# Macaron block in fp32: roots of two norms placed sooner, squares from feature tiles, 24 triples ahead of the pairs, output projection by four blocks, compression jobs spread

## The chip, the cores and the metric

One core of a Trainium2 chip. Its engines run side by side and wait for each other by semaphores: TensorE (PE) does matmuls, its weight loads are listed apart (PEld); VectorE (DVE) and ScalarE (ACT) do elementwise work, ScalarE also activations; GpSimd (POOL) helps with elementwise work; SyncE (SP) issues the DMAs. The metric is the device time of one execution, in microseconds (us).

## The reference

Batch 1, S = 512 tokens, D = 1024 features, all in fp32. One block: half of a SwiGLU FFN, a mixer, half of a second FFN, a final norm.

```
x = x + 0.5 * swiglu(rmsnorm(x, norm_ffn1), gate, up, down)          # D_FF = 2816
x = x + hybrid_mixer(rmsnorm(x, norm_mix), ...)
x = x + 0.5 * swiglu(rmsnorm(x, norm_ffn2), gate, up, down)
out = rmsnorm(x, norm_final)

rmsnorm(x, g) = x * rsqrt(mean(x*x) + eps) * g
swiglu(h) = (silu(h @ w_gate) * (h @ w_up)) @ w_down
```

The mixer projects h by `w_in` into queries, keys and values of 16 heads of 64. Heads 0 to 7 attend in blocks of 256 (MoBA). Heads 8 to 15 (NSA) sum three attentions with gates: over keys and values compressed by a small MLP (31 positions; the code calls its parts k/v `proj`, `hid`, `sec`), over selected blocks, and over a window. The 16 outputs are concatenated and multiplied by `w_out` (1024 x 1024).

## The kernel before

**Layout.** x lies in eight feature tiles `x0` to `x7` (128 features x 512 tokens). fp32 products are made of three matmuls of a rounded type (`mm3`, L86 to L88): high by high, high by low, low by high part. Every operand is split for it: ACT makes the high part (L80 for weights, L196 for other data), DVE the low part (L81, L197); in the mixer POOL takes L81 of small weights. For the norms, x times the gain is split into `xo` (`gained`, L122 on ACT and L123 on DVE), and the root R of a token is multiplied in later. Squares of x are summed over the feature tiles into `acc` (L134, L137 on ACT, the add L138), `sums_of_squares` adds over the partitions by matmuls with ones (`pr`, L144), `roots` gives 1/rms, and `rows_of_roots` spreads it over a 128x512 tile R (`pR`, L155, copied by ACT at L157).

**FFN.** D_FF is 22 columns f of 128. The first four f are `plain`: 16 steps of 12 matmuls (2.72 us of PE by the code's own table), eight with feature tiles 0 to 3 and eight with 4 to 7. Then `finish` makes h from the two banks: two products with R (L260), Silu, a product (L262), and `kept` splits h into high part (L224) and low part (L225). The other 18 f are taken two at a time by `pair`, seven products of sums of blocks in the manner of Strassen and Winograd (14 steps of 1.36 us). They need sums of x's blocks, which DVE makes out of x, the gain and R: `sums_of_x` (L186 to L190) and `blocks_of_x`, entered by `x_sums` at numbered plain steps. The weights' sums (`aw`, L288) and splits (L196, L197) are DVE and ACT work too. `down` multiplies four h by `w_down` in triples of matmuls (0.68 us): for a pair of output tiles d first k = 0, 1, 2 of both, then k = 3 of both; the bank is added to x at L464. There are 32 triples for the four plain h. `LEAD` of them come right behind the plain steps; the rest is mixed into the first pairs. So the steps are: plain, LEAD triples, then pairs mixed with triples.

**What sets the order.** Inside an FFN, PE's order is the list of steps (`go`), which also calls each step's loads, sums and splits 26, 12.8 and 8.6 us of PE ahead; the other engines' order, and all engines' in the mixer, comes from the Tile scheduler, from simulated times. A function attached to a step (`post`) is placed behind it: roots, rows of roots, sums of x, and in FFN1 `put_rows` and copies of bias tables.

**FFN1's roots** come from four tiles of x by tokens (`in_x`, 512 KB each), squared by ACT with a running sum (L510).

**Mixer.** A list of jobs (`pre`, `fill`, `last`) is run by `stream`, which loads the weights of a job two jobs ahead into three buffers and splits them before use. `pre` holds the first projections and the compression (`kproj`, `khid`, `ksec`, `vproj`, `vhid`, `vsec`) and values by tokens (`vn`, `vm`). Then come the heads, 8 to 15, then 0 to 7: each in chunks, of which scores (`ps_s`, L874, L875; bias and maximum L880; exponential L882; reciprocal L884; scaling by POOL L889), transposes (`ps_t`, L898; split L901, L902) and values (`po`, L92, L93; halves L829 to L833) lag by 0, 4 and 7 chunks. Between these, `run` takes pieces of the `fill` jobs to keep PE busy. The last fills are MoBA's queries and keys (`pp`; t L590, L592; aq L599; ak L606 and a DMA that shifts it across partitions), two projections for two heads. The output projection `w_out(d, k0, k1)` multiplies blocks k0 to k1 (two heads each) for tile d and adds the bank to x (L784); a job of it may start only when its heads are done. In the order of before there are 32 such jobs of two blocks: (4,6) and (6,8) are NSA's, (0,2) is MoBA's heads 0 to 3, and (2,4), heads 4 to 7, are the `last`, eight jobs of six matmuls. Behind the last job for d comes its `gained` and `squares` for FFN2.

## Time and profile before

| | us |
|---|---|
| median of 3 runs | 1030.15 (1029.23 to 1030.98) |
| the profiled execution's own time | 1029.65 |
| its span, first to last instruction | 1027.9 |
| PE busy | 983.8 (96%) |
| DVE, ACT, POOL busy | 769.0, 528.6, 140.0 |
| mean granted clock of PE | 0.986 |

How its lines are read: a timeline row has the start, the time, the engine, the line of the code, the operation, output <- input by the program's names, the shape, and in brackets how long the engine was idle just before it and what ended that. A row of groups has the count behind x, then busy us, mean ns of one, and idle us. A row by windows has, for PE, PEld, DVE, ACT and POOL, busy us and instructions, then PE's granted clock (1.00 is full), the DMA's share and GB/s.

### The profile page before, as it was taken

The numbers are of one execution on the slowest core, as the hardware profiler recorded it, in microseconds if no ns is written. First come the engines' busy times: TensorE is split into PE (matmuls) and PEld (weight loads), VectorE is DVE, ScalarE is ACT, GpSimd is POOL, SyncE is SP. The second block draws the span as 40 slices with busy tenths as digits, with TensorE's granted clock in tenths as the row PEclk, the third lists the DMA queues.
The fourth block names the chain that finished last, engine by engine and source line by source line (L and its number), as shares of the span: only waits on it lengthen the run. The fifth ranks groups of instructions, "written<-read, shape, count | busy, mean of one in ns | idle before, by whom it ended". The sixth has DMA issues, their size and how long they took to land.

```text
span 1027.9 us, 15964 instructions
## 1 busy us (share of the span) xinstructions
PE 983.8 (96%) x6088; PEld 866.3 (84%) x6088; DVE 769.0 (75%) x1242; ACT 528.6 (51%) x913; POOL 140.0 (14%) x184
## 2 busy tenths in 40 slices
PE   9969999999999998999999999896999999999996
PEld 7848999999999897787877787685899999999985
DVE  4995776777766586688698989969677777677745
ACT  7733444444444255467577876646344444444336
POOL 0000000000000040046443645600000000000002
PEclk9989999999999999999999999998999999999999
DMA  9527433233321126531011322552333333342202
GB/s 325 204 71 225 129 123 101 90 110 94 100 82 41 45 75 184 179 105 52 16 42 26 99 57 79 154 197 89 103 101 104 95 95 101 124 123 62 62 1 82
DMA packets 43569, 106.55 MB, mean 104 GB/s; under 512 B 9410, under 2 KB 18323, under 8 KB 43493
## 3 DMA queue, kind: packets, MB, share of 16 engines
q1 hardware_dynamic: 43204, 105.39, 32.4%
q8 instruction: 48, 0.79, 0.3%
q14 instruction: 29, 0.23, 0.1%
q10 hardware_dynamic: 288, 0.14, 0.1%
HBM read 100.08 MB, written 5.30 MB: 103 GB/s over the span
## 4 chain that ended last, share of the span: by engine, by line
PE 51%; DVE 7%; issue 2%; ACT 2%; DMA 2%; POOL 0%; ACTq 0%; DVEq 0%; POOLq 0%; SPq 0%
PE pd L87 4%; PE pd L88 4%; PE pd L86 4%; PE pu L86 3%; PE pu L87 3%; PE pu L88 3%; PE pp L86 3%; PE pp L87 3%; PE pp L88 3%; PE pw L86 3%; PE pw L88 2%; PE pw L87 2%; PE ps_t L898 2%; PE pgu L88 1%; PE pgu L86 1%
## 5 line engine op out<-in xcount | busy, mean ns | idle before, releaser
L196 ACT ACTIVATE sph<-aw 128x1024 fp32r<-128x1024 f32 x126 | 133.7, 1061 | 263.3 <-PE pu L87 117.4
L197 DVE TENSOR_TENSOR spl<-aw,sph 128x1024 fp32r<-128x1024 f32 x126 | 153.6, 1220 | 35.8 <-ACT sph L196 35.8
L87 PE MATMUL pd<-h,whi 128*128 128x512 f32 x336 | 135.5, 403 | 16.1 <-DVE h L225 16.1
L80 ACT ACTIVATE whi<-raw 128x1024 fp32r<-128x1024 f32 (+3 forms) x125 | 108.7, 872 | 71.5 <-PE pd L87 24.9
L86 PE MATMUL pd<-h,whi 128*128 128x512 f32 x336 | 134.5, 400 | 1.1 <-DVE x L464 0.7
L88 PE MATMUL pd<-h,wlo 128*128 128x512 f32 x336 | 133.2, 396 | 0.0
L86 PE MATMUL pu<-th,sph 128*128 128x256 f32 x432 | 120.5, 279 | 0.5
L88 PE MATMUL pu<-th,spl 128*128 128x256 f32 x432 | 120.1, 278 | 0.0
L87 PE MATMUL pu<-tl,sph 128*128 128x256 f32 x432 | 120.0, 278 | 0.0
L81 DVE TENSOR_TENSOR wlo<-raw,whi 128x1024 fp32r<-128x1024 f32 (+3 forms) x84 | 102.2, 1219 | 23.6 <-ACT whi L80 19.7
L288 DVE TENSOR_TENSOR aw<-aw 128x1024 f32<-128x1024 f32 x72 | 87.7, 1219 | 24.2 <-DMA aw<-in_wgu 24.1
L464 DVE SCALAR_TENSOR_TENSOR x<-pd,x 128x512 f32<-128x512 f32 x88 | 60.2, 687 | 50.8 <-PE pd L88 50.7
L86 PEld LDWEIGHTS pu<-th,sph 128*128 128x128 f32 x432 | 81.1, 188 | 6.8 <-ACT wc L304 2.3
L87 PEld LDWEIGHTS pu<-tl,sph 128*128 128x128 f32 x432 | 81.6, 189 | 4.3
L87 PEld LDWEIGHTS pd<-h,whi 128*128 128x128 f32 x336 | 64.4, 192 | 23.4 <-DVE h L225 18.6
L88 PEld LDWEIGHTS pu<-th,spl 128*128 128x128 f32 x432 | 81.1, 188 | 0.0
L88 PE MATMUL pw<-xo,spl 128*128 128x256 f32 x288 | 79.8, 277 | 0.0
L86 PE MATMUL pw<-xo,sph 128*128 128x256 f32 x288 | 79.8, 277 | 0.0
L87 PE MATMUL pw<-xo,sph 128*128 128x256 f32 x288 | 79.8, 277 | 0.0
L88 PEld LDWEIGHTS pd<-h,wlo 128*128 128x128 f32 x336 | 64.4, 192 | 14.2
L86 PEld LDWEIGHTS pd<-h,whi 128*128 128x128 f32 x336 | 64.1, 191 | 7.6 <-ACT h L224 1.1
L81 POOL TENSOR_TENSOR wlo<-raw,whi 128x256 fp32r<-128x256 f32 (+1 forms) x41 | 47.6, 1163 | 69.6 <-ACT whi L80 68.7
(252 smaller groups left out, 2462.4 us busy)
## 6 DMA issues: line engine op xcount, KB each, us to landing
aw<-in_wgu SPq DMA_DIRECT2D x72, 512.0 KB, 3.7
raw<-in_wd1a SPq DMA_DIRECT2D x20, 512.0 KB, 4.1
raw<-in_wd2a SPq DMA_DIRECT2D x20, 512.0 KB, 3.7
raw<-in_w_a SPq DMA_DIRECT2D x16, 512.0 KB, 3.6
raw<-in_wgu SPq DMA_DIRECT2D x15, 512.0 KB, 6.6
raw<-in_w SPq DMA_DIRECT2D x8, 512.0 KB, 3.9
raw<-in_w_o SPq DMA_DIRECT2D x32, 128.0 KB, 2.1
scr_t<-scr_r SPq DMA_DIRECT2D x8, 384.0 KB, 6.1
```

The lines of the kernel that those rows point to most:

```text
L80: nc.scalar.activation(hi[:, s], src[:, s], AF.Copy)
L81: (nc.gpsimd if side[0] else nc.vector).tensor_tensor(lo[:, s], src[:, s], f32(hi[:, s]), ALU.subtract)
L86: nc.tensor.matmul(p, w[0], v[0], start=first, stop=False, skip_group_check=again)
L87: nc.tensor.matmul(p, w[0], v[1], start=False, stop=False, skip_group_check=again)
L88: nc.tensor.matmul(p, w[1], v[0], start=False, stop=last, skip_group_check=again)
L196: nc.scalar.activation(hi, v, AF.Copy)
L197: nc.vector.tensor_tensor(lo, v, f32(hi), ALU.subtract)
L288: nc.vector.tensor_tensor(to, x, y, op)
L464: nc.vector.scalar_tensor_tensor(xs[d], p, 0.5, xs[d], ALU.mult, ALU.add)
L898: nc.tensor.transpose(p[:, wide:wide + 128], lps[qi][:, j * 128:(j + 1) * 128], ident)
```

## The change

1. `LEAD` is 24 for 8, in both FFNs.
2. FFN1's sums of squares are made from the feature tiles: `squares` for each of the eight (ACT, and the seven adds on DVE), then `pr`. The four token tiles, their loads and the input `x` go. `pr` is placed behind plain step 3, R's rows (`pR`) behind step 4 (before: 5), the sums of x from step 5 on (before: 6).
3. FFN2: `pr` behind step 2 (before 3), `pR` behind 3 (before 5), the sums of x from step 4 (before 6).
4. `put_rows` goes from the end of the lead triples to the 19th pair step, the bias copies from pair steps 4 + 5i to 26 + 3i.
5. The compression's hidden jobs are spread among other jobs of `pre`, their bank has another tag, `vsec` is last.
6. The output projection has 16 jobs of four blocks: (4,8) for each d, in the fill at i = 2, and (0,4) for each d as the `last`. There is one add into x per job, and one split of 128x512 weights in place of two of 128x256.

```diff
-LEAD = 8
+LEAD = 24
-    def x_sums(ffn):
-        return [(at, lambda k=k, part=part: part(k)) for k, ats in enumerate(((6, 6), (8, 8), (10, 10), (13, 15)))
+    def x_sums(ffn, first):
+        return [(at, lambda k=k, part=part: part(k))
+                for k, ats in enumerate(((first, first), (first + 1, 8), (first + 3, 10), (first + 5, 15)))
                 for at, part in zip(ats, (ffn.sums_of_x, ffn.blocks_of_x))]
...
-        tokens = [ffn.raw().rearrange("p a b c -> p (a b c)") for _ in range(NT)]
-        for i in range(NT):
-            nc.sync.dma_start(tokens[i], A["x"][i * 128:(i + 1) * 128])
...
-        def squares_of_tokens():
-            for i in range(NT):
-                nc.scalar.activation(tokens[i], tokens[i], AF.Square, accum_out=ss[:, 0, i:i + 1])
-            roots(0, ss[:, 0])
+        def squares_of_x():
+            for k in range(NK):
+                squares(tmp, k, "tmp", 3, nc.vector)
...
         steps = ffn.plain(range(FP), [
-            (1, squares_of_tokens), (5, lambda: rows_of_roots(0, "mm")), (8, make_rows),
-            *x_sums(ffn)])
+            (0, squares_of_x), (3, lambda: roots(0, sums_of_squares("mm"))), (4, lambda: rows_of_roots(0, "mm")),
+            (8, make_rows), *x_sums(ffn, 5)])
         fills = ffn.down(A["wd1a"][0], range(FP), half_added, "mm", 2)
         steps += fills[:LEAD]
-        steps[-1].post.append(put_rows)
...
+        pairs[18].post.append(put_rows)
         for i in range(8):
-            pairs[4 + 5 * i].post.append(lambda i=i: copied_bias(i))
+            pairs[26 + 3 * i].post.append(lambda i=i: copied_bias(i))
...
-                        p.append(pt("mm", "pc"))
+                        p.append(pt("t", "pc"))
...
-                if k1 == 4:
+                if k0 == 0:
                     got["x", d] = gained(d, 2)
...
-        pre = [kproj, *vn, proj(10, nsa_k("ks")), *khid[:2], vm[0], *khid[2:], vproj, vm[1], ksec, vm[2],
-               *vhid, vsec, vm[3], proj(12, nsa_q(0))]
+        pre = [kproj, *vn, khid[0], proj(10, nsa_k("ks")), khid[1], vm[0], khid[2], vproj, khid[3], vm[1], ksec,
+               vhid[0], vm[2], vhid[1], vhid[2], vm[3], vhid[3], proj(12, nsa_q(0)), vsec]
...
             if i == 2:
-                fill += [w_out(d, 4, 6) for d in range(NK)]
-        fill += [w_out(d, k, k + 2) for k in (6, 0) for d in range(NK)]
-        last = [w_out(d, 2, 4) for d in range(NK)]
+                fill += [w_out(d, 4, 8) for d in range(NK)]
+        last = [w_out(d, 0, 4) for d in range(NK)]
...
         steps = ffn.plain(range(FP), [
-            (3, lambda: roots(2, sums_of_squares("mm"))), (5, lambda: rows_of_roots(2, "mm")), *x_sums(ffn)])
+            (2, lambda: roots(2, sums_of_squares("mm"))), (3, lambda: rows_of_roots(2, "mm")), *x_sums(ffn, 4)])
```

How it moves instructions is seen at three places. In the order's rows names carry the tile's number; the changed kernel's lines stand a few lower (L784 is L781 there, L874 L871, L898 L895, L902 L899).

DVE in FFN1, before, up to the low part of the last of the four plain h (`h_575` and `h_617` are h2 and h3; the rows of h0 and h1 stand 15 and 10 rows ahead of `h_575`):

```order
L260 TENSOR_TENSOR t_611<-pgu_329,R_100 128x512
L260 TENSOR_TENSOR t_611<-pgu_370,R_100 128x512
L288 TENSOR_TENSOR aw_423<-aw_425,aw_423 128x1024
L189 SCALAR_TENSOR_TENSOR xb_546<-xb_546 128x256
L197 TENSOR_TENSOR tl3_130<-xa_545,th3_129 128x256
L225 TENSOR_TENSOR h_575<-t_569,h_574 128x512
L262 TENSOR_TENSOR t_611<-t_611 128x512
L288 TENSOR_TENSOR aw_443<-aw_423,aw_443 128x1024
L197 TENSOR_TENSOR tl3_130<-xb_546,th3_129 128x512
L225 TENSOR_TENSOR h_617<-t_611,h_616 128x512
```

The same place now (`h_547`, `h_592` and `h_629` are h1, h2 and h3):

```order
L262 TENSOR_TENSOR t_586<-t_586 128x512
L81 TENSOR_TENSOR wlo_647<-raw_511,whi_646 128x1024
L225 TENSOR_TENSOR h_547<-t_541,h_546 128x512
L189 SCALAR_TENSOR_TENSOR xb_491<-xb_491 128x256
L197 TENSOR_TENSOR tl3_130<-xa_490,th3_129 128x256
L288 TENSOR_TENSOR aw_570<-aw_550,aw_570 128x1024
L262 TENSOR_TENSOR t_623<-t_623 128x512
L225 TENSOR_TENSOR h_592<-t_586,h_591 128x512
L197 TENSOR_TENSOR tl3_130<-xb_491,th3_129 128x512
L225 TENSOR_TENSOR h_629<-t_623,h_628 128x512
```

The low parts of h1, h2 and h3 now stand close together; h1's has the sums and splits of x's blocks ahead of it that stood behind it before.

PE in the mixer, before, at the last head's transposes (`ps_t`) and values (`po`); `pw` is the output projection, and `o60` to `o71` are outputs of heads finished long before:

```order
L898 MATMUL ps_t_6667<-ident_84,lpn_6535 128x128
L898 MATMUL ps_t_6667<-ident_84,lp_6556 128x128 x2
L93 MATMUL po_6705<-tl_6626,vm_4222 128x512
L92 MATMUL po_6705<-th_6645,vm_4223 128x384
L93 MATMUL po_6705<-tl_6646,vm_4223 128x384
L86 MATMUL pw_6882<-o60_5562,whi_6850 128x512
L87 MATMUL pw_6882<-o61_5563,whi_6850 128x512
L88 MATMUL pw_6882<-o60_5562,wlo_6851 128x512
L86 MATMUL pw_6882<-o70_5968,whi_6850 128x512
L87 MATMUL pw_6882<-o71_5969,whi_6850 128x512
L88 MATMUL pw_6882<-o70_5968,wlo_6851 128x512
L898 MATMUL ps_t_6696<-ident_84,lpn_6575 128x128
```

Now, at the last head's scores and transposes (`kvn_6738` and `kvn_6739` are the output of heads 4 and 5, halves of one block):

```order
L871 MATMUL ps_s_6746<-ak_6576,aq_6590 128x384
L872 MATMUL ps_s_6746<-ak_6578,aq_6590 128x384
L895 MATMUL ps_t_6755<-ident_84,lpn_6634 128x128
L895 MATMUL ps_t_6776<-ident_84,lpn_6634 128x128
L871 MATMUL ps_s_6767<-ak_6576,aq_6590 128x512
L872 MATMUL ps_s_6767<-ak_6578,aq_6590 128x512
L895 MATMUL ps_t_6755<-ident_84,lpn_6671 128x128
L895 MATMUL ps_t_6776<-ident_84,lpn_6671 128x128
L87 MATMUL pw_6861<-kvn_6739,whi_6505 128x512
L88 MATMUL pw_6861<-kvn_6738,wlo_6506 128x512
L87 MATMUL pw_6886<-kvn_6739,whi_6538 128x512
L88 MATMUL pw_6886<-kvn_6738,wlo_6539 128x512
```

The jobs (0,2) and (6,8) that stood between are gone from there; what is left is the beginning of the last jobs, up to the block whose heads are done.

DVE at the end of the mixer, before: the add of the last blocks into x (L784), and the low part of x times the gain (L123):

```order
L784 TENSOR_TENSOR x0_70<-pw_7022,x0_70 128x512
L784 TENSOR_TENSOR x1_71<-pw_7041,x1_71 128x512
L123 SCALAR_TENSOR_TENSOR xo_7031<-x0_70,gcol_69,xo_7030 128x512
L784 TENSOR_TENSOR x2_72<-pw_7062,x2_72 128x512
L123 SCALAR_TENSOR_TENSOR xo_7050<-x1_71,gcol_69,xo_7049 128x512
L784 TENSOR_TENSOR x3_73<-pw_7083,x3_73 128x512
L123 SCALAR_TENSOR_TENSOR xo_7071<-x2_72,gcol_69,xo_7070 128x512
L784 TENSOR_TENSOR x4_74<-pw_7104,x4_74 128x512
```

Now:

```order
L781 TENSOR_TENSOR x0_70<-pw_6861,x0_70 128x512
L781 TENSOR_TENSOR x1_71<-pw_6886,x1_71 128x512
L123 SCALAR_TENSOR_TENSOR xo_6876<-x0_70,gcol_69,xo_6875 128x512
L123 SCALAR_TENSOR_TENSOR xo_6901<-x1_71,gcol_69,xo_6900 128x512
L781 TENSOR_TENSOR x2_72<-pw_6913,x2_72 128x512
L123 SCALAR_TENSOR_TENSOR xo_6928<-x2_72,gcol_69,xo_6927 128x512
L781 TENSOR_TENSOR x3_73<-pw_6940,x3_73 128x512
L123 SCALAR_TENSOR_TENSOR xo_6955<-x3_73,gcol_69,xo_6954 128x512
```

Engine and rows are of one kind as before; what has changed is that each add stands for a bank of 12 matmuls in place of six, and that a first add of the same tile, for the blocks (0,2), no longer comes ahead.

More of the change, by code (lines that the diff above doesn't have):

```diff
@@ L1173, in _laid_out @@
         "gcol": c(np.stack([g[0].reshape(NK, 128).T for g in (norm_ffn1, norm_mix, norm_ffn2)], axis=1)),
-        "x": c(x[0]), "wgu1": _gate_up(w_ffn1_gate[0], w_ffn1_up[0]),
+        "wgu1": _gate_up(w_ffn1_gate[0], w_ffn1_up[0]),
         **dict(zip(("wd1a", "wd1b"), _down(w_ffn1_down[0]))),
```

## The prediction

> **What bounds the kernel now.** I read the page's head first, then busy time in stretches of 25 us, then TensorE's timeline for its gaps, then what the other engines do inside those gaps.
>
> ```profile
> span 1027.9 us, 15964 instructions
> PE 983.8 (96%) x6088; PEld 866.3 (84%) x6088; DVE 769.0 (75%) x1242; ACT 528.6 (51%) x913; POOL 140.0 (14%) x184
> ```
>
> TensorE (PE) is busy for 983.8 of 1027.9 us: the bound is its work plus 44.1 us of gaps. The change takes no matmul of weight away, so it can only win gaps, open new ones, or change the clock in them. Where they are:
>
> ```profile
> 0.00:25.00 25.00, 22.79 (x88) 17.82 (x89) 11.99 (x22) 18.49 (x30) 0.81 (x8) 1.00 0.92 324
> 50.00:75.00 25.00, 16.40 (x72) 11.50 (x70) 24.36 (x36) 8.62 (x14) 0.00 (x0) 0.80 0.20 65
> 400.00:425.00 25.00, 21.90 (x111) 17.64 (x110) 16.38 (x25) 12.11 (x18) 0.00 (x0) 1.00 0.50 156
> 552.00:668.00 116.00, 109.23 (x577) 89.71 (x576) 105.02 (x242) 84.31 (x198) 64.60 (x87) 1.00 0.31 89
> 648.00:668.00 20.00, 15.94 (x66) 11.61 (x65) 18.75 (x19) 14.45 (x24) 14.86 (x13) 1.00 0.58 177
> 700.00:725.00 25.00, 17.12 (x62) 13.11 (x62) 24.64 (x36) 10.95 (x18) 0.00 (x0) 0.80 0.22 73
> 750.00:775.00 25.00, 24.86 (x181) 22.95 (x180) 17.66 (x20) 10.92 (x15) 0.00 (x0) 1.00 0.37 116
> ```
>
> Columns: window and its length, then busy us of PE, weight loads, DVE, ACT and POOL, PE's granted clock, DMA share and GB/s. In the body of an FFN PE has no gap worth naming (750:775). One hole stands in each FFN where the plain part ends (8.6 and 7.9 us, the clock down to 0.80 on average, DVE full), 3.1 us in the compression (400:425), and 6.8 us in the last 116 us of the mixer, 4.06 of them in its tail (648:668). These are the places that the change touches.
>
> **FFN1: roots sooner, LEAD 24.** The hole on PE, and what DVE does meanwhile:
>
> ```profile
> 54.97 0.50 PE L87 MATMUL pd<-h,whi 128*128 128x512 f32 x1 [1.42 <-DVE h L225]
> 58.85 0.80 PE L87 MATMUL pd<-h,whi 128*128 128x512 f32 x1 [2.92 <-DVE h L225]
> 65.13 0.80 PE L87 MATMUL pd<-h,whi 128*128 128x512 f32 x1 [3.88 <-DVE h L225]
> 60.00:64.00 4.00, 0.86 (x2) 0.29 (x1) 4.00 (x6) 1.03 (x2) 0.00 (x0) 0.50 0.37 131
> 24.60 1.05 PE L155 MATMUL pR<-ident,rc 128*128 128x128 f32 x8
> 26.32 0.75 DVE L186 SCALAR_TENSOR_TENSOR xa<-x,gcol,R 128x512 f32<-128x512 f32 x1 [0.42 <-ACT R L157]
> 26.99 0.75 DVE L186 SCALAR_TENSOR_TENSOR xb<-x,gcol,R 128x512 f32<-128x512 f32 x1
> 64.39 0.68 DVE L225 TENSOR_TENSOR h<-t,h 128x512 fp32r<-128x512 f32 x1
> 67.33 0.68 DVE L225 TENSOR_TENSOR h<-t,h 128x512 fp32r<-128x512 f32 x1
> ```
>
> The gaps wait for the low parts of h (L225): the third, h2, is made at 64.39, PE resumes at 65.13. From the first xa (26.32) DVE never pauses until past 67.33, so h2's time is R plus the DVE work queued ahead of it. The order says what becomes of that queue. Its rows from the first xa to h1, h2 and h3 cost 32.4, 38.9 and 41.9 us before and 36.5, 39.5 and 40.7 after (row by row at the spacing of rows in this trace; 26.32 to 26.99 is 0.67 for such a row). R comes sooner by less than the one step (2.7 us) that pR moves: the root's sums are eight matmuls more on PE (0.95 us by the row of FFN2's below), and two squares of ACT now stand ahead of a split that step 0 needs, one 0.63 each:
>
> ```profile
> L137 ACT ACTIVATE sq<-x 128x512 f32<-128x512 f32 x7 | 4.4, 627 | 2.6 <-DVE x L784 2.5
> 673.68 0.95 PE L144 MATMUL pr<-ones_f,acc 128*128 128x1 f32 x8
> ```
>
> So pR comes some 0.9 us sooner (2.7 − 0.95 with overlap − about 1.0), and xa at 25.4. Then h1 is ready at 61.9 (before 58.8), h2 at 64.9 (before 65.1), h3 at 66.1 (before 68.0). Each group of 24 triples needs all four h's, and the first that needs h2 is the third triple, so the longer lead cannot start work earlier: the hole keeps its end, within 0.2 us. The delay of step 0 costs nothing while the hole covers it, otherwise 1.0. The seven DVE adds of squares fall into the first 25 us, where DVE is busy for only 11.99; without that cover they are 7 × 0.6 = 4.2. The 2 MB of tokens no longer loaded are 2.1 MB / 324 GB/s = 6.5 us of transfers in a window with PE at 22.79 of 25: the most to win there is 2.2, and only if R moves with it. Against it, 16 more triples end their pairs of banks through L464 with two banks only (estimate 0.3 per FFN and octet, 0.6), and the first pairs meet a DVE with less slack (0.3). FFN1: **loss 0.7**, from −1.5 to +2.2 (gain).
>
> **FFN2: the same hole, without squares to add.**
>
> ```profile
> 682.27 0.75 DVE L186 SCALAR_TENSOR_TENSOR xa<-x,gcol,R 128x512 f32<-128x512 f32 x1
> 718.07 0.68 DVE L225 TENSOR_TENSOR h<-t,h 128x512 fp32r<-128x512 f32 x1
> 714.06 0.80 PE L87 MATMUL pd<-h,whi 128*128 128x512 f32 x1 [4.79 <-DVE h L225]
> 718.80 0.80 PE L87 MATMUL pd<-h,whi 128*128 128x512 f32 x1 [3.09 <-DVE h L225]
> ```
>
> pR moves two steps (5.4 us) and pr one; xa comes about 4.4 us sooner, bounded by a split ahead of it on DVE. But the rows from the first xa to h2's low part are 39.5 us in the new order where they were 36.6. So h2 comes 4.4 − 2.9 = 1.5 sooner; less the 0.9 for the lead as in FFN1, **gain 0.6**, from −1.0 to +2.5.
>
> **Compression jobs spread.**
>
> ```profile
> 400.85 0.50 PE L86 MATMUL pp<-xo,whi 128*128 128x512 f32 x1 [0.47 <-ACT whi L80]
> 403.02 1.20 PE L86 MATMUL pv<-whi,xo 128*128 128x512 f32 x4 [1.43 <-ACT whi L80]
> 424.28 1.19 PE L86 MATMUL pv<-whi,xo 128*128 128x512 f32 x4 [0.98 <-ACT whi L80]
> ```
>
> All three wait for a weight split whose raw buffer the loader, two jobs ahead, got late. At 400 four short hidden jobs stood in a row; spread, each gets a longer neighbour that hides its 512 KB load: the 0.47 + 1.43 and a small gap before them (0.3) go, 2.2. The 0.98 stays: in the new order vhid0 is followed by vm2 and vhid1 closely, with short jobs still side by side. **Gain 2.2**, from 0 (the wait moves to another job) to 3.7 (all of 400:425 with 0.6 around it).
>
> **Output projection by four blocks, and its tail.** Rows on which this part rests:
>
> ```profile
> L784 DVE TENSOR_TENSOR x<-pw,x 128x512 f32<-128x512 f32 x32 | 21.7, 681 | 3.3 <-PE pw L88 3.0
> L902 DVE TENSOR_TENSOR tl<-ps_t,th 128x384 fp32r<-128x384 f32 x23 | 12.6, 548 | 0.6 <-ACT th L901 0.5
> L880 DVE CUSTOM_DVE_ANT_0 lp<-ps_s,tb 128x512 f32<-128x512 f32 x10 | 6.8, 677 | 1.9 <-PE ps_t L898 1.9
> L833 DVE TENSOR_TENSOR kvn<-to,u 64x512 fp32r<-64x512 f32 x8 | 6.6, 828 | 0.9 <-ACT u L832 0.9
> 605.75 0.23 PE pp L87
> 606.78 0.33 PE ps_t L898 x3
> 617.80 2.44 DMA ak<-ak
> L123 DVE SCALAR_TENSOR_TENSOR xo<-x,gcol,xo 128x512 fp32r<-128x512 f32 x7 | 9.6, 1370 | 0.2 <-ACT xo L122 0.2
> 656.53 0.47 PE L86 MATMUL pw<-kvn,whi 128*128 128x512 f32 x1 [0.78 <-DVE x L784]
> 663.10 0.50 PE L88 MATMUL pgu<-xo,wlo 128*128 128x512 f32 x1 [2.10 <-DVE wlo L81]
> 484.78 0.79 PE L874 MATMUL ps_s<-kvn,aq 128*128 128x512 f32 x1 [1.51 <-DVE m L880]
> 484.00:488.00 4.00, 3.22 (x12) 2.69 (x13) 3.94 (x14) 1.48 (x5) 1.16 (x3) 0.57 0.00 0
> ```
>
> *The tail.* Today each feature tile has 6 matmuls last (6 × 0.23 = 1.4 us of PE) beside one add (0.68) and one L123 (1.37, beside POOL) on DVE, 2.05: DVE is slower, and PE waits (656.53). With 12 matmuls PE has 2.7 us per tile: the two balance. Of 4.06 us idle I keep 0.8 for the first tiles and the L81 that starts FFN2. **Gain 3.3**, from 1.5 (the 2.10 of 663.10 stays, and half the rest) to 3.6.
>
> *Relief.* 16 adds fewer: 16 × 0.68 = 10.9 us less DVE work. In 552:668 DVE is busy for 105 of 116 us. The idle time of PE there ahead of the tail is 6.8 − 4.1 = 2.7; **gain 2.0**, from 0.5 to 2.7.
>
> *What is taken from heads 0 to 5.* Work that filled PE while heads waited is now in the last job. In one stretch the order keeps 15.7 us of PE's attention work with five w_out matmuls (1.1 us) in it where there were more than seven us of them. Such a stretch without fill is seen at 484:488: PE 3.22 of 4, and 1.51 of idle in one piece. With 10 to 12% idle: **loss 1.8**, from 0 to 3.
>
> *Heads 6 and 7.* The last two projections (48 matmuls, 10.9 us) stand in a block; the moment it ends is E. Behind it PE has, up to the next w_out matmul that waits for heads 6 and 7, 33 transposes (3.7 us at 0.11), 33 value and 16 score matmuls (6.9 by their widths, at 0.23 for 512) and 18 of w_out (4.1): 14.6 us. DVE has 47 rows: splits, scores, sums and halves (L902, L880, L833 and their like), some 21 us by their durations, and 17 once 0.08 is taken off for the overlap of neighbours. They are a chain: E, the split of k, its copy by DMA (2.44), scores, exponentials, transposes, values, halves. So PE waits at least 17.1 − 14.6 = 2.5 us; at most, with the DMA and two ACT/PE hand-overs of about 0.9 in series (21.3), 6.7. I take 4.5, and 1.0 for the clock: at 484:488 it fell to 0.57 in a sparse stretch, where 3 us of PE at half speed would be 1.5 more. Before, 24 jobs of w_out covered this chain. **Loss 5.5**, from 2.5 to 8.
>
> The Trainium skill, TensorE: Matmul & The Clock Gate, section "HAM oscillation — how this bites in real kernels", gives the rule "no PE-idle gaps >~3.4µs". By it the clock would hold here, as no single wait in my chain is that long, and the loss at heads 6 and 7 would be 4.5. This trace disagrees: the clock was 0.57 behind a stretch whose longest gap is 1.51 us.
>
> *The rest.* Put_rows and bias copies move within FFN1's pairs, where PE is full and DVE has slack (750:775 shows 17.66 of 25 for the like part): nothing; without that cover three copies of 0.6 each, 1.8.
>
> **Sum.** −0.7 + 0.6 + 2.2 + 3.3 + 2.0 − 1.8 − 5.5 = +0.1 us. The profiled execution took 1029.65 us (span 1027.9), 0.5 under the median of 1030.15. Less 0.1, the median stays at **1030.1**.
>
> **The rivals.**
> A, faster. DVE is the limit in the mixer, and 10.9 us less work on it is worth more than its fill. For it: DVE 105 of 116 us. Against it: PE idles there for only 6.8, so nothing beyond that is to be had. Heads 6 and 7 then cost the lower end, 2.5, heads 0 to 5 nothing: −0.7 + 0.6 + 2.2 + 3.3 + 2.7 − 2.5 = 5.6 gained, 1024.5.
> B, slower. Heads 6 and 7 without fill: at PE's w_out behind block E. If the DVE chain takes its serial length (21.3), with the clock at half behind it, PE loses 8 instead of 5.5, and heads 0 to 5 lose 3.0: +0.1 − 2.5 − 1.2 = −3.6, 1033.7; should the split at 663.10 stay too, 1035.5. It decides from a chain of about 19 us on. For it: the fill is gone from the order. Against: DVE has fewer rows elsewhere, so it may come to E with less behind it.
> C, the change doesn't do what it says. Roots are sooner, the h's are not: that is my forecast for FFN1. If the added DVE rows between xa and h2 in FFN2 come to 4.4 as well, its 0.6 becomes −0.9, the whole 1031.6, still within the forecast.
> D, the holes close. If the two holes shrink by all that R gains (0.9 and 4.4) because the later rows on DVE turn out cheaper, 1030.1 − 1.6 − 2.9 = 1025.6. Against: DVE is full through both, so its rows have to be done first.
>
> **How the numbers follow.** What a measurement of this kernel can tell from no change is about 0.2%, 2.06 us. The forecast, with C, has 0.34 (its own range 1028.0 to 1032.2); A 0.23 and D 0.11, together 0.34 for faster; B 0.32. The bounds of the terms, taken as independent, combine to some 4.5 us either way (the root of the squares of 1.5, 1.7, 1.8, 1.1, 1.1, 1.5 and 2.7); A's 1024.5 and a little beyond B's 1035.5 make the range 1024.3 to 1036.0.
>
> **What would show it.** Right: h2's L225 in FFN1 within a microsecond of 65, PE's gaps at 55 to 65 still over 8 us in sum; FFN2's last gap ending about 1.5 us earlier after its start; gaps at 400 gone; in the tail no wait for L784 (now with two blocks more) over 0.5; and, between the last pp matmul and the first w_out of heads 6 and 7, 4 to 6 us of idle PE with the clock below 1. Wrong: PE idle under 2 us there, or a hole in an FFN that shrinks by over 2 us, or one that opens at put_rows' new place; then A or D was the case, or the sum missed a place altogether.

## The result and the profile after

The changed kernel takes 1038.62 us (median of four, 1035.94 to 1040.46) against 1030.57 us for the kernel before: ratio 1.0078, 95% interval 1.0051 to 1.0106. Measured again beside other runs (e5 below) it is 1.0069, 1.0048 to 1.0091. It is slower by some 7.5 us, outside the range of 1024.3 to 1036.0; the forecast was no change that can be measured. Executions that took over 1.5% longer than the fastest of their kernel (one of e2, one of e10) are left out throughout.

The head of the page after, and two windows (columns as in the prediction). The second FFN starts 11.3 us later than before (671.7 for 660.4), so the prediction's 552:668 and 648:668 are moved by as much; the last is the mixer's tail:

```profile
span 1035.6 us, 15887 instructions
PE 991.0 (96%) x6096; PEld 868.3 (84%) x6096; DVE 759.1 (73%) x1232; ACT 526.2 (51%) x897; POOL 138.8 (13%) x169
...
563.30:679.30 116.00, 108.80 (x547) 87.25 (x546) 87.37 (x207) 78.67 (x168) 57.49 (x67) 0.99 0.30 90
659.30:679.30 20.00, 20.00 (x90) 16.57 (x89) 15.98 (x15) 13.56 (x19) 12.46 (x10) 1.00 0.63 202
```

The idle time of PE is as before: 1035.6 − 991.0 = 44.6 us, where it was 44.1. PE's busy time has grown by 7.2, though only the eight small matmuls of the squares' sums are new. So part of the loss lies in matmuls that ran at a lower clock or stand wider apart. The comparison that shows it cuts both traces at the same events: the first matmul of the plain steps, the first triple, the first pair product, the first projection, the first scores, and the same in the second FFN. Before:

```profile
6.70:53.20 46.50, 45.70 (x202) 36.63 (x200) 37.70 (x65) 34.84 (x57) 0.00 (x0) 1.00 0.73 270
53.20:71.90 18.70, 10.10 (x31) 5.81 (x29) 18.66 (x27) 6.42 (x9) 0.00 (x0) 0.73 0.17 57
71.90:363.70 291.80, 290.85 (x2018) 268.26 (x2018) 205.23 (x234) 121.79 (x160) 4.69 (x6) 1.00 0.33 103
363.70:443.80 80.10, 76.12 (x421) 64.10 (x419) 55.72 (x79) 43.52 (x69) 8.58 (x9) 1.00 0.48 148
...
660.40:708.20 47.80, 45.70 (x210) 37.74 (x208) 39.98 (x63) 28.07 (x43) 4.96 (x4) 1.00 0.52 175
708.20:724.90 16.70, 8.82 (x26) 6.25 (x25) 16.34 (x24) 4.92 (x8) 0.00 (x0) 0.69 0.17 63
724.90:1019.30 294.40, 294.12 (x2049) 271.26 (x2047) 204.25 (x236) 127.06 (x175) 3.80 (x3) 1.00 0.28 87
```

After:

```profile
6.00:56.40 50.40, 48.64 (x209) 38.83 (x209) 45.37 (x77) 33.83 (x55) 0.00 (x0) 0.97 0.61 212
56.40:83.80 27.40, 19.91 (x74) 14.59 (x73) 19.50 (x28) 7.51 (x11) 0.00 (x0) 0.88 0.25 77
83.80:369.60 285.80, 281.63 (x1975) 259.83 (x1974) 200.82 (x230) 120.91 (x159) 4.62 (x6) 1.00 0.33 101
369.60:449.40 79.80, 76.39 (x409) 64.72 (x408) 56.36 (x77) 43.42 (x68) 10.58 (x10) 0.98 0.48 149
...
671.70:717.40 45.70, 45.67 (x210) 37.78 (x209) 40.49 (x65) 26.12 (x42) 2.94 (x3) 1.00 0.48 162
717.40:742.40 25.00, 19.53 (x74) 14.66 (x73) 16.89 (x24) 7.05 (x9) 0.00 (x0) 0.86 0.29 84
742.40:1027.20 284.80, 283.15 (x2001) 262.53 (x1999) 199.27 (x230) 124.99 (x173) 3.75 (x3) 1.00 0.28 86
```

| stage | before, us | after, us | difference |
|---|---|---|---|
| FFN1, plain steps | 46.5 | 50.4 | +3.9 |
| FFN1, lead triples and pairs (together, as triples moved between them) | 310.5 | 313.2 | +2.7 |
| first projections and compression | 80.1 | 79.8 | −0.3 |
| heads and output projection | 216.6 | 222.3 | +5.7 |
| FFN2, plain steps | 47.8 | 45.7 | −2.1 |
| FFN2, lead triples and pairs | 311.1 | 309.8 | −1.3 |

(Heads: from 443.8 to 660.4, and from 449.4 to 671.7. The rest, start and end, is −0.9.) PE's gaps behind these numbers, from its timeline of the changed kernel:

```profile
11.57 0.77 PE L87 MATMUL pgu<-xo,whi 128*128 128x512 f32 x1 [0.74 <-DVE xo L123]
63.69 0.80 PE L87 MATMUL pd<-h,whi 128*128 128x512 f32 x1 [5.11 <-DVE h L225]
66.70 0.79 PE L87 MATMUL pd<-h,whi 128*128 128x512 f32 x1 [1.36 <-DVE h L225]
97.37 0.39 PE L86 MATMUL pu<-th,sph 128*128 128x256 f32 x1 [0.82 <-ACT wc L304]
121.89 0.39 PE L86 MATMUL pu<-th,sph 128*128 128x256 f32 x1 [0.82 <-ACT wc L304]
158.27 0.50 PE L86 MATMUL pd<-h,whi 128*128 128x512 f32 x1 [1.75 <-DVE x L465]
160.00 0.39 PE L86 MATMUL pu<-th,sph 128*128 128x256 f32 x1 [0.77 <-DVE t L319]
392.72 0.50 PE L88 MATMUL pp<-xo,wlo 128*128 128x512 f32 x1 [2.15 <-DVE wlo L81]
...
652.45 0.50 PE L87 MATMUL pw<-kvn,whi 128*128 128x512 f32 x1 [1.30 <-DVE kvn L830]
723.98 0.80 PE L87 MATMUL pd<-h,whi 128*128 128x512 f32 x1 [4.45 <-DVE h L225]
755.98 0.39 PE L86 MATMUL pu<-th,sph 128*128 128x256 f32 x1 [0.82 <-ACT wc L304]
```

Two kinds are new and stand where the kernel before has no gap in this list: 0.82 us, twice in the first pair group of each FFN (the fourth, at 778.93, is alike), and 1.75 with 0.77 in the second group of FFN1. The first kind is a copy on ACT that came too late. ACT's timeline at that place:

```profile
95.77 1.06 ACT L196 ACTIVATE sph<-aw 128x1024 fp32r<-128x1024 f32 x1 [1.82 <-PE pu L87]
96.73 0.58 ACT L304 ACTIVATE wc<-pu 128x512 f32<-128x512 f32 x1
```

The product of step S2 ends and its bank `pu` has to be copied out (L304) before S3 may write it. A split of 1.06 us stands ahead of the copy on ACT. In the kernel before, two triples (1.4 us) follow that step in the first pair group; with 24 triples gone ahead, one (0.68) is left there. Two don't cover all of it either. PE's timeline has the end of the second triple and the first matmul of S3 in the kernel before:

```profile
86.89 0.39 PE L88 MATMUL pd<-h,wlo 128*128 128x512 f32 x1
87.42 0.39 PE L86 MATMUL pu<-th,sph 128*128 128x256 f32 x1
```

From start to start these are 0.53 us, where matmuls of a triple follow each other every 0.23; in the changed kernel it is 1.22 (96.15 to 97.37). So each of the four waits costs 0.69 us more than before.

The second kind starts on SP. Its queue, and the DVE instruction that it holds up:

```profile
128.46 15.66 SPq L519 DMA_DIRECT2D cb<-scr_c  x21
...
148.64 0.35 SPq L281 DMA_DIRECT2D aw<-in_wgu  x1
```

```profile
155.25 1.22 DVE L288 TENSOR_TENSOR aw<-aw 128x1024 f32<-128x1024 f32 x1 [10.70 <-DMA aw<-in_wgu]
```

Behind `put_rows` 40 copies of bias rows are issued, 8 of `scr_t<-scr_r` and 32 small ones of `cb<-scr_c`; 21 of these in a row stand on SP's queue for 15.7 us. Weight loads stand behind them, DVE waits 10.7 us for one, and behind DVE's waiting add stands the one that frees PE's bank (L465).

### The profile page after: what moved, and what is told of

The parts are those of the page before. It is cut to its first block, busy times and chain, and to the rows that moved or that the text cites. A ratio compares the mean times of both kernels' runs of the same rounds, so it can differ in the third digit from the quotient of the medians.

```text
span 1035.6 us, 15887 instructions
## 1 busy us (share of the span) xinstructions
PE 991.0 (96%) x6096; PEld 868.3 (84%) x6096; DVE 759.1 (73%) x1232; ACT 526.2 (51%) x897; POOL 138.8 (13%) x169
## 4 chain that ended last, share of the span: by engine, by line
PE 52%; DVE 5%; ACT 3%; issue 2%; DMA 1%; ACTq 0%; DVEq 0%; SPq 0%
PE pd L87 4%; PE pd L86 4%; PE pd L88 4%; PE pu L86 3%; PE pu L88 3%; PE pu L87 3%; PE pw L87 3%; PE pw L88 3%; PE pw L86 3%; PE pp L88 3%; PE pp L86 3%; PE pp L87 3%; PE ps_t L895 2%; PE pgu L86 1%; PE pgu L87 1%
## 5 line engine op out<-in xcount | busy, mean ns | idle before, releaser
L80 ACT ACTIVATE whi<-raw 128x1024 fp32r<-128x1024 f32 (+3 forms) x109 | 105.7, 971 | 109.3 <-PE pd L87 41.5
L81 DVE TENSOR_TENSOR wlo<-raw,whi 128x1024 fp32r<-128x1024 f32 (+3 forms) x83 | 100.0, 1207 | 20.0 <-ACT whi L80 19.2
L465 DVE SCALAR_TENSOR_TENSOR x<-pd,x 128x512 f32<-128x512 f32 x88 | 60.3, 688 | 59.1 <-PE pd L88 59.1
L87 PE MATMUL pw<-xo,sph 128*128 128x256 f32 x288 | 79.8, 277 | 0.0
L87 PEld LDWEIGHTS pw<-xo,sph 128*128 128x128 f32 x288 | 54.3, 189 | 2.7
```

What stands on the lines that cost most here:

```text
L80: nc.scalar.activation(hi[:, s], src[:, s], AF.Copy)
L81: (nc.gpsimd if side[0] else nc.vector).tensor_tensor(lo[:, s], src[:, s], f32(hi[:, s]), ALU.subtract)
L87: nc.tensor.matmul(p, w[0], v[1], start=False, stop=False, skip_group_check=again)
L465: nc.vector.scalar_tensor_tensor(xs[d], p, 0.5, xs[d], ALU.mult, ALU.add)
```

## The experiments

Ratios are to the kernel before, run beside it on the same chip, with 95% intervals. The changed kernel's own, 1.0069 and 1.0078, are what each undone part is held against; "theory" is the reading of the trace above.

**e1: LEAD = 8.**

```diff
-LEAD = 24
+LEAD = 8
```

> The changed kernel with LEAD = 8 again, all else as changed. Theory (thin fill): with 24 triples ahead only 8 are left for the first pair group of each FFN, and twice there PE waits 0.82 us for a bank that ACT copies out (L304) behind a split; four such gaps go, and the two holes stay as long as they are: about 1034 to 1036 (3 us less). Rival (the lead closes the holes): with 8 the work ahead of the hole's end is missing, so the holes grow and the time is 1040 or more. No effect would say that both are wrong.

1029.90 us, ratio 0.9994 (0.9976 to 1.0012): the whole loss goes, more than twice what was expected. In its trace all four 0.82 gaps and both at 158 and 160 are gone, and the first FFN from the first triple on takes 309.0 us, as these windows show (313.2 in the changed kernel):

```profile
54.70:70.80 16.10, 8.80 (x25) 6.03 (x24) 14.24 (x22) 5.35 (x8) 0.00 (x0) 0.68 0.21 65
70.80:363.70 292.90, 292.56 (x2024) 268.75 (x2023) 205.92 (x236) 122.86 (x161) 4.67 (x6) 1.00 0.34 102
```

The hole keeps its idle time (8.8 of 16.1 busy, 7.3 idle; 7.5 in the changed kernel). The rival, that the lead closes the holes, is out. `put_rows` stands as late here as in the changed kernel, and DVE still waits for the weights behind its copies; but PE has no gap from it:

```profile
149.27 1.23 DVE L288 TENSOR_TENSOR aw<-aw 128x1024 f32<-128x1024 f32 x1 [7.97 <-DMA aw<-in_wgu]
```

**e2: bias rows and their copies where they were.**

```diff
         steps += fills[:LEAD]
+        steps[-1].post.append(put_rows)
...
-        pairs[18].post.append(put_rows)
-            pairs[26 + 3 * i].post.append(lambda i=i: copied_bias(i))
+            pairs[4 + 5 * i].post.append(lambda i=i: copied_bias(i))
```

> The changed kernel with put_rows behind the lead triples and the copies of bias rows at pair steps 4 + 5i as before. Theory (queue): the 32 small copies cb<-scr_c occupy SP's issue queue for 21 us right after the bias rows, two weight loads are issued behind them, DVE waits 10.7 us for one, and PE loses 1.75 + 0.77 us at 158 and 160; with the old places the DVE wait of over 5 us and both gaps go: 2 to 3 us less, 1035 to 1036.5, and a narrower spread of the runs. Rival (the DMA engines, not the order of issue, are full there): the gaps stay somewhere in the first pairs, within 1 us of the changed kernel.

1035.12 us, 1.0037 (1.0020 to 1.0054): 3 to 4 us less. The gaps at 158 and 160 are gone, one of 0.71 (a split on DVE) is new at 110. The spread didn't narrow (1032.5 to 1038.4). With `LEAD` at 24 the place of `put_rows` matters; with 8 (e1) it cost PE nothing.

**e3: the (4,8) jobs behind all projections.**

```diff
-            if i == 2:
-                fill += [w_out(d, 4, 8) for d in range(NK)]
+        fill += [w_out(d, 4, 8) for d in range(NK)]
```

> The changed kernel with the eight (4,8) jobs of the output projection behind all projections instead of ahead of those for heads 6 and 7. Theory (no fill behind the last projections): PE gets 96 matmuls of fill (22 us) for the time in which heads 6 and 7 go through DVE, ACT and POOL; of the lost 4.0 us idle and some 4 us at the half clock at 634 to 656 most goes: 6 to 8 us less, 1030.5 to 1032.5. Rival (the chain of heads 6 and 7 on DVE and ACT ends last whatever PE does): the end of the mixer moves by under 2 us, 1036.5 or more, as the adds of the late jobs lengthen the chain.

1036.08 us, 1.0053 (1.0036 to 1.0069): 2 us less, not 6 to 8. The stage of the heads shrinks from 222.3 to 218.8. What stays is the very end of head 7:

```profile
649.85 0.50 PE L87 MATMUL pw<-kvn,whi 128*128 128x512 f32 x1 [1.42 <-DVE kvn L830]
640.00:656.00 16.00, 13.85 (x59) 10.26 (x58) 7.99 (x13) 7.72 (x14) 5.17 (x4) 0.89 0.15 45
```

The fill is used up before the last halves (L830) are made, and the clock falls there (0.89 over 16 us) as it did without fill.

**e4: the output projection in two-block jobs as before.**

```diff
             if i == 2:
-                fill += [w_out(d, 4, 8) for d in range(NK)]
-        last = [w_out(d, 0, 4) for d in range(NK)]
+                fill += [w_out(d, 4, 6) for d in range(NK)]
+        fill += [w_out(d, k, k + 2) for k in (6, 0) for d in range(NK)]
+        last = [w_out(d, 2, 4) for d in range(NK)]
...
-                if k0 == 0:
+                if k1 == 4:
```

> The changed kernel with the output projection in 32 jobs of two blocks, ordered as before. Theory: heads 6 and 7 are covered again (8 us gained), the tail's waits for the adds return (4 us lost): 1034 to 1035.5. Rival (the blocks are not what costs the mixer; the new order of the compression shifts the heads): within 1.5 us of the changed kernel.

1035.17 us, 1.0047 (1.0028 to 1.0066): 2 to 3 us less. The heads' stage is 214.9 us, 7.4 less than with four blocks; FFN2 gives 3 back (its plain steps and hole start with the tail's waits). 16 more adds on DVE cost nothing there.

**e5: the changed kernel again**, beside e6 to e8.

> The changed kernel once more, unaltered, beside the runs below. Theory: about 8 us over the kernel before (1.0078, as first measured), with a spread of the runs of 4 us or more, since in some executions the clock falls to half at 12 to 15 us (PE idle for 1.4 us of the four before) and at 393, and in others not. Rival (the first measurement was of a bad chip): within 4 us of the kernel before.

1038.54 us, 1.0069 (1.0048 to 1.0091). The four executions lie 2.7 us apart, not 4.

**e6: FFN1's roots from token tiles.**

```diff
+        tokens = [ffn.raw().rearrange("p a b c -> p (a b c)") for _ in range(NT)]
+        for i in range(NT):
+            nc.sync.dma_start(tokens[i], A["x"][i * 128:(i + 1) * 128])
...
-            (0, squares_of_x), (3, lambda: roots(0, sums_of_squares("mm"))), (4, lambda: rows_of_roots(0, "mm")),
+            (1, squares_of_tokens), (4, lambda: rows_of_roots(0, "mm")),
```

> The changed kernel with FFN1's sums of squares from four token tiles as before; R's rows stay behind step 4. Theory (squares crowd ACT): the gaps of 0.30, 0.33 and 0.74 us at 8 to 12 us go, the clock stays full in the first 25 us, eight matmuls (0.95) go, so the plain part ends 2 to 4 us sooner and with it R and the hole: 2.5 to 4 us less than the changed kernel. Rival (the hole covers it): h's low parts are set by DVE's queue, the hole grows by what the start gains, under 1 us.

1037.61 us, 1.0061 (1.0039 to 1.0082): 0.9 less than e5, not clear of the noise, and the rival's side. The start's gaps go and the clock is full, but:

```profile
23.28 1.13 PE L155 MATMUL pR<-ident,rc 128*128 128x128 f32 x8 [1.36 <-DVE rc L149]
...
64.98 0.79 PE L87 MATMUL pd<-h,whi 128*128 128x512 f32 x1 [3.10 <-DVE h L225]
```

PE waits for the root at step 4, and h's third low part lets it go at 64.98, where the changed kernel stood at 66.70 for its last. The plain steps end 2.0 us sooner than in e5, FFN1 only 1.2.

**e7: the compression's jobs in the old order.**

```diff
-        pre = [kproj, *vn, khid[0], proj(10, nsa_k("ks")), khid[1], vm[0], khid[2], vproj, khid[3], vm[1], ksec,
-               vhid[0], vm[2], vhid[1], vhid[2], vm[3], vhid[3], proj(12, nsa_q(0)), vsec]
+        pre = [kproj, *vn, proj(10, nsa_k("ks")), *khid[:2], vm[0], *khid[2:], vproj, vm[1], ksec, vm[2],
+               *vhid, vsec, vm[3], proj(12, nsa_q(0))]
```

> The changed kernel with the order of the compression's jobs and its bank's tag as before. Theory: the gaps at 399 to 403 (2.4 us) come back and the 2.15 at 392 goes; the compression takes 80 us again where it took 77.7 (clock full) or 79.7 (clock half for some us), and the heads behind it keep their time: 0 to +2.5 us against the changed kernel. Rival (the new order of jobs also costs the heads): 2 us or more faster.

1044.31 us, 1.0135 (1.0094 to 1.0177): 5.8 slower than e5. So the new order gains, and more than was expected. In the trace the compression takes 82.5 us (79.1 in e5), with the old gaps back (0.89, 1.52 and 1.33); the longest:

```profile
411.20 1.41 PE L86 MATMUL pv<-whi,xo 128*128 128x512 f32 x4 [1.52 <-ACT whi L80]
```

The profiled execution is 7.5 us longer than e5's: 3.4 in this stage, 1.4 in the heads (222.6 for 221.2), 0.7 in FFN2's plain steps, and 1.9 up to the end of FFN1, whose instructions are the same (what differs there is the clock; see the last section). The four executions of e7 lie 10 us apart. What of the 5.8 us between the medians belongs to the order alone isn't told; the 3.4 are what the stage itself shows.

**e8: FFN2's roots at the old steps.**

```diff
-            (2, lambda: roots(2, sums_of_squares("mm"))), (3, lambda: rows_of_roots(2, "mm")), *x_sums(ffn, 4)])
+            (3, lambda: roots(2, sums_of_squares("mm"))), (5, lambda: rows_of_roots(2, "mm")),
...
```

(The sums of x go back to steps 6, 8, 10, 13 and 15.)

> The changed kernel with the second FFN's roots and sums of x at the places of before. Theory: R is 4.4 us later, h's low parts follow, the hole of FFN2 grows by 2 to 3.5 us: 2 to 3.5 us slower than the changed kernel. Rival (DVE's queue, not R, sets the h's): no difference beyond 1 us, or faster.

1041.14 us, 1.0102 (1.0067 to 1.0138): 2.6 slower than e5, as expected. From the first triple to the end FFN2 takes 314.0 us in place of 310.2, all of it in the hole:

```profile
722.82 0.58 PE L87 MATMUL pd<-h,whi 128*128 128x512 f32 x1 [4.80 <-DVE h L225]
727.56 0.79 PE L87 MATMUL pd<-h,whi 128*128 128x512 f32 x1 [3.31 <-DVE h L225]
```

**e13: LEAD = 24 as the only edit of the kernel before.**

```diff
-LEAD = 8
+LEAD = 24
```

> The kernel before with LEAD = 24 as its only edit (put_rows stays behind the lead, the bias copies at pair steps 4 + 5i). Theory (the lead costs by itself): two waits of 0.82 us for a copied bank in each FFN, the rest by weight loads issued behind the bias copies in FFN1; FFN1 3 to 5 us and FFN2 2 to 2.5 us longer, ratio 1.004 to 1.007. Rival (it costs only beside the later place of put_rows or beside the sooner roots): ratio 0.998 to 1.002.

1034.32 us, 1.0024 (1.0011 to 1.0037): slower by itself, by 2.5 us, less than I gave it. From the first pair product on two 0.82 gaps stand in each FFN; no gap at 158. From the first plain step to the end FFN1 and FFN2 take 3.0 and 2.8 us longer (360.0 and 361.9 us; 357.0 and 359.1 before, from the events as above). These are one profiled execution of each kernel, and more than the ratio gives. The first of the four gaps:

```profile
98.58 0.39 PE L86 MATMUL pu<-th,sph 128*128 128x256 f32 x1 [0.82 <-ACT wc L304]
```

**e14: LEAD = 24, the eight triples left behind the copies.** Four stand behind each step whose bank is copied next, none elsewhere.

```diff
+            if len(fills) == 8:
+                weight = [1 if i % 14 == 7 else 0 for i in range(len(steps))]
             for i, s in enumerate(steps):
```

> The changed kernel (LEAD = 24), in which the eight triples left for the first pair group stand four and four behind the steps whose bank is to be copied, none elsewhere. Theory (the wait is a copy of 0.58 us behind a split of 1.06 on ACT, with one triple of 0.68 us to cover it): the four gaps of 0.82 go, 3 us less than the changed kernel: ratio to before 1.0035 to 1.005. Rival (thin fill leaves DVE and ACT without time at whatever step): the gaps turn up at the other banks' copies and the ratio stays at 1.006 to 1.008.

1034.06 us, 1.0022 (1.0007 to 1.0038): 4.5 to 5.5 us less than the changed kernel, a little more than expected. All four 0.82 gaps are gone, at the same LEAD and with the same eight triples, and none came up at another bank; of the two gaps in the second group 0.70 and 0.77 are left. That is the mechanism shown: not how much fill there is, but that one triple doesn't cover the split and the copy on ACT. The wait for weights behind the bias copies stays:

```profile
153.15 1.22 DVE L288 TENSOR_TENSOR aw<-aw 128x1024 f32<-128x1024 f32 x1 [9.65 <-DMA aw<-in_wgu]
```

**e16: the 32 copies from ACT's queue.**

```diff
-                nc.sync.dma_start(
+                nc.scalar.dma_start(
                     cb[a * 16:(a + 1) * 16, j],
```

> The changed kernel with the 32 copies cb<-scr_c issued from ACT's queue instead of SP's. Theory (weight loads wait behind them in SP's queue): the weights land in time, DVE's wait of 10.7 us and PE's 1.75 and 0.77 us at 158 and 160 go; the issues take ACT's time instead, some of which may show as waits on ACT: 0 to 2.5 us less. Rival (the DMA engines are full, or the landing of so many small packets is what is late): DVE still waits 8 us or more for the weights.

1038.02 us, 1.0062 (1.0045 to 1.0078): nothing gained that can be told, but the cause moves as the theory says. The add that waited 10.7 us starts at 152.17 in place of 155.25, after a wait of 1.72, and 158 and 160 are free. Part of the shorter wait is that DVE comes to it 5.9 us later. For ACT now has the issues in its queue, and a split that it makes late costs PE elsewhere:

```profile
125.82 1.06 ACT L196 ACTIVATE sph<-aw 128x1024 fp32r<-128x1024 f32 x1 [3.74 <-DMA cb<-scr_c]
```

```profile
140.94 0.38 PE L88 MATMUL pw<-xo,spl 128*128 128x256 f32 x1 [1.50 <-DVE spl L197]
```

The load that the add waits for lands 4.7 us behind its issue in the changed kernel and 3.3 here, so the landing can't be the 10.7 us. It is the order of issue, not the DMA engines, that held the weights back.

**e9 to e12 and e15: what gained, put together.** e9 is e1 with e4's jobs; e10 has the output projection as (4,6) at i = 2, (6,8) behind all projections and (0,4) last; e11 is e1 with e3's order. e12 is the kernel before with two parts of the change: FFN2's roots sooner and the new order of the compression. e15 is e12 with (4,8) behind all projections and (0,4) last.

e10, against the changed kernel with LEAD = 8:

```diff
             if i == 2:
-                fill += [w_out(d, 4, 8) for d in range(NK)]
+                fill += [w_out(d, 4, 6) for d in range(NK)]
+        fill += [w_out(d, 6, 8) for d in range(NK)]
```

e15, against e12:

```diff
-            if i == 2:
-                fill += [w_out(d, 4, 6) for d in range(NK)]
-        fill += [w_out(d, k, k + 2) for k in (6, 0) for d in range(NK)]
-        last = [w_out(d, 2, 4) for d in range(NK)]
+        fill += [w_out(d, 4, 8) for d in range(NK)]
+        last = [w_out(d, 0, 4) for d in range(NK)]
```

> The changed kernel with LEAD = 8 and the output projection in two-block jobs as before. Theory (the losses are separate and add): 8 and 3 to 4.5 us less than the changed kernel, 4 to 5 less than the kernel before: ratio 0.995 to 0.997. Rival (they overlap; a hole or wait elsewhere takes up the second gain): like LEAD = 8 alone, 0.9985 to 1.0005.

> LEAD = 8; output projection as (4,6) in the fill at i = 2, (6,8) behind all projections, (0,4) as the last, so that the tail has 12 matmuls per add and heads 6 and 7 have half of the fill of before. Theory (heads need fill, the tail needs long jobs): the tail's 2 to 4 us are kept and most of heads 6 and 7 is covered: 0 to 2 us under the run with two-block jobs throughout. Rival (24 short jobs were needed, not 8): 1 to 3 us over it.

> LEAD = 8 and the (4,8) jobs behind all projections. Theory: the last waits of head 7's values at the end (0.68 and 1.42 us, and the clock at half behind them) stay, so this is 1 us over the two-block run and 2 to 2.5 under LEAD = 8 alone. Rival (what (4,8) covers is all there is): equal to the two-block run or below.

> The kernel before with two parts of the change alone: FFN2's roots sooner, and the new order of the compression. Theory (FFN1's new roots bring nothing, the squares on ACT and DVE only trouble the start): 0 to 1.5 us under the two-block run with LEAD = 8, ratio to before 0.993 to 0.9965, with the narrower spread of the kernel before. Rival (FFN1's roots from feature tiles do bring something, 2 MB of loads fewer): 1 us or more over it.

> The kernel before with FFN2's roots sooner, the new order of the compression, and the output projection by four blocks with the (4,8) jobs behind all projections. Theory (what gained, together): 0 to 1.5 us under the kernel with two-block jobs, ratio to before 0.993 to 0.995. Rival (the mixer loses by the late jobs what the tail gains): 0.9945 to 0.997.

| run | median, us | ratio | interval |
|---|---|---|---|
| e9, LEAD 8, two blocks | 1026.92 | 0.9956 | 0.9942 to 0.9971 |
| e10, LEAD 8, mixed jobs | 1027.09 | 0.9954 | 0.9937 to 0.9970 |
| e11, LEAD 8, (4,8) late | 1026.06 | 0.9945 | 0.9924 to 0.9965 |
| e12, FFN1 as before, two blocks | 1025.26 | 0.9946 | 0.9927 to 0.9964 |
| e15, FFN1 as before, (4,8) late | 1025.61 | 0.9938 | 0.9923 to 0.9953 |

All five beat both kernels; between them the intervals overlap, so e10 to e12 don't tell two blocks from four, nor token tiles from feature tiles, and the small differences that I expected among the five aren't shown. The traces of e12 and e15 say why the blocks make none: with (4,8) late the heads take 3.8 us longer (218.6 for 214.8), and FFN2 4.5 less (353.6 for 358.1). e15 is some 6 us under the kernel before, with three of the change's six parts, the third of them (the output projection) with its (4,8) jobs put later.

## Why the prediction was wrong, step by step

**LEAD, the step that failed.** I gave the longer lead 0.6 for banks and 0.3 for DVE in each FFN. It costs 2.5 us by itself (e13) and nearly 8 in the changed kernel (e1). The term for banks was about right: inside the lead, PE loses 0.37 us at each of two changes of bank in each FFN, 0.74 for 0.6. The first in FFN1 (0.49 and 0.34 us from start to start in place of 0.23):

```profile
72.33 0.50 PE L86 MATMUL pd<-h,whi 128*128 128x512 f32 x1
72.67 0.40 PE L87 MATMUL pd<-h,whi 128*128 128x512 f32 x1
```

What was missing is another mechanism: I asked whether DVE has slack in the first pairs, and it has, but the wait is ACT's copy of a bank behind a split (four gaps of 0.82), which the two triples at that step had mostly covered. I counted fills by their number and not by the step behind which they stand.

**put_rows, priced at nothing.** I named PE's fullness and DVE's slack as its cover and priced three copies on DVE. I counted none of the 40 DMAs that it releases on SP's queue, nor the weight loads behind them. They cost 2.5 us in the trace and 3 to 4 by e2. The prediction's own sign of being wrong, a hole that opens at put_rows' new place, is this one. Before, the same copies ran at 72 to 107, beside the 24 triples mixed into the first pairs.

Both are needed for the 8 us. With `LEAD` at 8 the late copies cost PE nothing (e1), and with the early copies `LEAD` at 24 leaves no gap at 158 (e13). Counted from start to start, the four waits cost 2.8 us more than before, the two gaps in the second group 2.5 and the banks of the lead 1.5, together 6.8; from the first triple on, e1's stages are shorter than the changed kernel's by 4.2 in FFN1 and by some 2 in FFN2. The rest, 1 to 2 us, isn't placed; a fall of the clock behind the gaps at 158, seen in other executions (last section), may be part of it. In the profiled executions e1 has the full clock at 12 to 15 us and at 392 to 400, where the changed kernel had 0.50 and 0.74 to 0.83; but the instructions up to 50 us are the same, so I don't count this for LEAD.

**FFN1's hole: right in what sets it, wrong by its size.** The hole stayed, as forecast, since h's low parts hang on R and on DVE's queue. I had h2's at 64.9; it was made at 65.97, and the gaps sum to 7.3 and not over 8. DVE's rows from xa to there took 38.7 (39.5 forecast). That is 0.8 less, as for h1 and h3, and in the kernel before it is 0.6 to 0.9 less: the row sums were too long by some 0.8 throughout and their differences right. But R was not 0.9 sooner: xa started at 27.30, 1.0 later than before, since the start lost PE 1.4 us in gaps and fell to half the clock. (In e8, with the same FFN1 and the full clock, it was 25.97, 0.35 sooner than before.)

```profile
27.30 0.75 DVE L186 SCALAR_TENSOR_TENSOR xa<-x,gcol,R 128x512 f32<-128x512 f32 x1 [1.59 <-ACT R L157]
65.97 0.68 DVE L225 TENSOR_TENSOR h<-t,h 128x512 fp32r<-128x512 f32 x1
12.00:15.00 3.00, 3.00 (x8) 2.32 (x8) 3.00 (x5) 3.00 (x6) 0.00 (x0) 0.50 0.95 303
```

**FFN2: 1.5 forecast for the roots, 2.6 measured (e8).** From FFN2's first matmul, xa comes 5.4 us sooner than in e8 (14.1 for 19.5), where 4.4 was forecast; the rows from there to h2's low part take 38.7 us in place of 35.8, the 2.9 more that were forecast. So the term that was mis-sized is R's place; the mechanism held.

**Compression: 2.2 forecast, 2.4 in the stage where the clock held (by e7 5.8, of which 3.4 are seen in the stage).** The gaps at 400 went. One came that I had not named, 2.15 at 392: L81's add stands behind eight adds of L693 (4.34 us) on DVE. The stage in the profiles of before and after differs by 0.3 only, since the clock fell in the latter (0.79 at 392 to 400). Where it held throughout the stage, in e1, e2, e4, e8 and e9, the new order takes 77.6 to 77.8 us, 2.4 under the 80.1 of before; in the ten others with it, where the clock fell once, 79.1 to 79.8. So 2.2 was right for the gaps, and a fall of the clock had no term. In e7 the old order takes 82.5 with one such fall (0.86 at 412 to 424).

**Heads 6 and 7: right.** 4.5 of idle time and 1.0 for the clock were forecast; between 632 and 656 PE was idle for 5.0 us, with the clock at 0.94:

```profile
632.00:656.00 24.00, 19.00 (x91) 13.10 (x90) 17.61 (x45) 16.45 (x39) 6.38 (x10) 0.94 0.10 28
```

(In e5's profiled execution, of the same kernel, the clock held there.)

**Tail: right** (3.3 forecast). In 659:679 PE has no idle time, where the same stretch of the kernel before (648:668) had 4.06; against two-block jobs (e4) FFN2 is 2.9 us shorter. **Relief of DVE: mostly missing.** DVE has 17.7 us less to do in 563:679 than in 552:668 before. PE is idle there for 7.2 us, 5.0 of them at heads 6 and 7; the other 2.2 stand against 2.7 outside the tail before. That is 0.5 less, where 2.0 was forecast. Heads 6 and 7, heads 0 to 5 and the relief were to cost 5.3 together; against e4 the heads' stage is 7.4 us longer. How much of this difference is heads 0 to 5, for which 1.8 was forecast, isn't told apart. All parts of the output projection sum to −2.0 in the forecast and to −2.7 by e4 (1.0047 against 1.0073, the mean of the two).

Of the rivals, B was the nearest in sign, yet for another reason: heads 6 and 7 cost what the forecast gave them.

## What to carry to other kernels

Fill that keeps the bound engine busy has to be counted at the step where a bank is copied out or a chain runs, not as a total: eight triples behind the right steps left no wait for a copied bank, where the same eight spread out left four of 0.82 us. An edit that moves a function moves its DMAs too; read what stands behind them in the issue queue, and behind the engine that waits for those loads. And a part that relieves an engine is worth only the waits that this engine ended.

## What the runs showed of the hardware

The clock falls, or not, on the same instructions. At 12 to 15 us the granted clock is 0.50 to 0.55 in six of the thirteen profiled kernels that take FFN1's squares from feature tiles (the changed kernel, e2, e3, e5, e9, e16) and 1.00 in the other seven; their instructions up to there are alike, and the four microseconds before have PE busy for about 2.5, in gaps of under 1 us. In the five with token tiles (3.2 to 3.6 of 4 busy) it never fell. The row of e1, beside the changed kernel's above:

```profile
12.00:15.00 3.00, 3.00 (x15) 2.46 (x14) 3.00 (x6) 3.00 (x6) 0.00 (x0) 1.00 1.02 314
```

15 matmuls in place of 8 in the same 3 us. The Trainium skill, TensorE: Matmul & The Clock Gate, section "What's actually happening", says of the gate's window that "it's free-running — it doesn't reset when your kernel starts", which would let the same gaps cost or not cost. The traces agree with that. They don't agree with the rule on gaps that the prediction quotes: in the changed kernel the clock fell behind gaps of 0.74 at most.

What a fall costs isn't told by its own stretch alone. In the kernels with feature tiles FFN1's plain steps took 50.3 to 50.9 us with the fall at 12 to 15, and 47.9 to 48.7 without it. Yet FFN1 as a whole took 363.7 us in both profiled executions of the changed kernel, which had the fall, and 364.5, 365.1 and 366.4 in e4, e7 and e8, which have the same FFN1 and had none there. In these three PE came sooner to the weights at 158, which came no sooner; its first gap there was 2.81, 2.94 and 2.27 us in place of 1.75, and the clock fell behind it, to 0.60, 0.64 and 0.50. The changed kernel and e8:

```profile
160.00:164.00 4.00, 4.00 (x29) 3.79 (x30) 4.00 (x6) 1.57 (x3) 0.00 (x0) 1.00 0.55 154
160.00:164.00 4.00, 3.49 (x14) 3.39 (x15) 4.00 (x6) 1.36 (x2) 0.00 (x0) 0.50 0.63 201
```

So a gap can cost more than its length, in some executions of a kernel and not in others, and one profiled execution can't tell its mean.
